# The gates of an mLSTM layer as float32 products in column quarters, moved from behind val(0) to behind the plain tiles

## The chip, the cores and the metric

The kernel runs on one NeuronCore of one Trainium2 chip. Its engines are TensorE (PE in the profile; PEld is its weight load), VectorE (DVE), ScalarE (ACT), GpSimd (POOL) and the queue engine SyncE (SP), which here issues nearly all transfers. The metric is the device time of one execution in microseconds. The kernel before has a median of 2676.51 us over three runs (2673.63 to 2676.99).

## The reference

One inference step of a decoder layer, for a prompt of 1024 rows and a group of 8 sample rows (1032 columns in the kernel, which keeps everything transposed), width 1024, all in float32:

```
x = LN1(ALPHA*x + 0.5*SwiGLU_1(x))
z = x @ w_in + b_in        # columns: q k v o-gate | i-gate(4) f-gate(4) | B C h | merge gates a, b
log_i = z[i-gate];  log_f = log_sigmoid(z[f-gate])
y_a = (HeadLN(mLSTM(q, k, v, log_i, log_f)) * sigmoid(o)) @ w_a
y_b = (B * conv3(C * h)) @ w_b
x = LN2(ALPHA*x + (sigmoid(g_a)*y_a + sigmoid(g_b)*y_b) @ w_mix)
x = LN3(ALPHA*x + 0.5*SwiGLU_2(x));  x = LN4(ALPHA*x + sigmoid(x @ w_pg) * (p @ w_pp))
```

The mLSTM is the chunked, stabilised form: cumulative sums of log_f, running maxima and exponentials of them weight the products of q, k and v. The part that this document is about is small: eight columns of z (four input gates, four forget gates), and the arithmetic that turns them into the decay factors of all chunks and heads.

## The kernel before, in words

Large products are done in the split form: each float32 operand is held as a high part in float32r and a low part, and a product is three float32r matmuls, high x high, high x low, low x high (L172 to L174 for plain tiles, L432 to L434 for the others). The 1032 columns are cut into four blocks (BLK4) of 256, 260, 256 and 260; most weights are taken in pairs of 128-column tiles, and such a pair is computed by a seven-product scheme (`pair`, L438) over two column halves: 14 steps of 12 matmuls each, with sums of x parts (`xsums`, L219) and of weight parts (`wcomb`, L249) prepared on DVE, ACT and POOL. After each step, `pair` takes one entry off the list `beside` (L436, L481) and issues what is in it: so small work of other kinds is threaded through the pairs.

All engines work in order. Which order that is, a planner of the framework decides when the kernel is built: it walks the program with a cost model and puts on each engine what is ready, by priority in program order. Tiles with one name share a fixed number of buffers: `mm` 4, `pn` 1 and `aux` 3 PSUM tiles, `raw` 3 and `tmp` 4 SBUF tiles. `unit_ps` (L103) takes every fifth tile from `pn`, the others from `mm`. `sg_pair` (L752) hands out two pairs of large tiles in turn, and `slot()` (L132) the ring of nine weight slots.

The stage concerned follows the first feed-forward part. Lines L958 to L971 compute LN1 for the four column blocks in the order 0, 2, 1, 3; its rows `rp` stay in SBUF in float32 and are split into high and low parts. L974 to L981 compute the first q and k tiles plainly (16 units of 24 matmuls). Then x is stored (L984), the weights of the first pair are loaded and combined, and the sums of x are formed: those of the first half before conv(0), those of the second half (`late_sums`, L229) as the first four entries of `beside`. conv(0) (L1227) is three pairs (C, h and B) with a short convolution (`conv_y`, L927) between the second and the third; val(0) (L1228) is one pair, whose result is transposed block by block (L1043) and stored; then come the gates (L1057 to L1088); then conv(1), q, k, val and so on for three more heads.

The gates before: the eight weight columns are split into high and low parts, laid side by side into a 128-column weight tile (i high at 0, f high at 32, i low at 64, f low at 96), and multiplied with the split parts of x, 16 or 24 matmuls for a column block, 80 in all (L1083 to L1085). The blocks of x are read from the parts of the seven-product scheme, some as sums of two parts, hence 24. The result `g0` (100 rows used) is transposed (L808, L815), and the rows that belong to high and low weights are added (`both`, L800). `gate_math` (L797) is a generator: each of its steps issues a few small instructions, and 22 entries of `beside` run it, so that it stands beside conv(1), which follows. Its results are needed by `decays` (L1090, from `gscr`) behind conv(1), and later by the chunks and the sample rows. Two of its inputs and outputs go through DRAM (L887 gscr, L914 state_m, L923 and L924 sscr and wkb).

Float32 matmuls that are not split are in the kernel too: the mean and variance of LN (L385, L407), the cumulative sums of the gates (L848, L850), and the products of the sample rows with their state (L1202), which put four 128x32 weight tiles into the four column quarters of TensorE and sum the four row groups of the result by a product with a selection matrix `sel` (L1210).

Of the kernel before, what the change touches and what calls it, by code (L numbers as in the profile page):

```python
# [8 lines left out]
F32 = mybir.dt.float32  # L9
R = mybir.dt.float32r  # L10
I32 = mybir.dt.int32
AF = mybir.ActivationFunctionType
OP = mybir.AluOpType
PSUM = bass.MemoryType.PSUM

D = 1024
# [7 lines left out]
Q0, K0, V0, O0, I0 = 0, 1024, 2048, 3072, 4096  # L24
# [6 lines left out]
BN = (256, 260)  # L31
BM = 260
BLK4 = [(i // 2 * HW + i % 2 * BN[0], BN[i % 2]) for i in range(4)]
# [3 lines left out]
def F_(ap):  # L37
    return ap.bitcast(F32)


def ccol(c):

    return c // 4 * HW + c % 4 * 128
# [6 lines left out]
def smp(t):  # L50

    return v2(t)[:, :, 512:516]
# [6 lines left out]
def p24(t):  # L59
    return t.rearrange("p (b r) -> p b r", r=4)  # L60
# [3 lines left out]
def layer_kernel(ctx: ExitStack, tc: tile.TileContext, I, O):  # L64
    nc = tc.nc
    V, S, G, T, DQ = nc.vector, nc.scalar, nc.gpsimd, nc.tensor, nc.sync

    sb = ctx.enter_context(tc.tile_pool(name="sb", bufs=1))
    rawp = ctx.enter_context(tc.tile_pool(name="raw", bufs=3))
# [17 lines left out]
    def sreg(dt=F32):  # L87

        t = sb.tile([128, 8 * BM], dt, name="sreg", tag="sreg")
        if dt == F32:  # L90
            SR[:] = [t]
            SN["v"] = [[t[:, i * HW + c:i * HW + c + n] for c, n in BLK4[:2]] for i in range(4)]
        return t

    def tmp(n=BM):
        return tmpp.tile([128, BM], F32, name="tmp", tag="tmp")[:, :n]
# [3 lines left out]
    def mm(n=512):  # L100
        return psp.tile([128, 512], F32, name="mm", tag="mm", bufs=NMM)[:, :n]

    def unit_ps(n=512):  # L103

        turn["n"] += 1
        return mm(n) if turn["n"] % 5 else psp.tile([128, 512], F32, name="pn", tag="pn", bufs=1)[:, :n]
# [3 lines left out]
    def aux(n=512):  # L110
        return psp.tile([128, 512], F32, name="aux", tag="aux", bufs=7 - NMM)[:, :n]


    ident = sb.tile([128, 128], F32, name="ident")
# [17 lines left out]
    def slot():  # L132
        s = ring["slots"][ring["i"] % len(ring["slots"])]
        ring["i"] += 1
        return gen(s, R)
# [47 lines left out]
    def bs(t, b, blk=BLK):  # L183
        c0, n = blk[b]
        return t[:, c0:c0 + n]
# [16 lines left out]

    def xparts(X7, j, kp):
        t = X7[j][kp // 2]
        return t[:, 2 * (kp % 2)], t[:, 2 * (kp % 2) + 1]
# [139 lines left out]
    def bcol(c0, m):  # L345
        return col(c0 // 128 + m) if c0 < 4096 else col(32 + (c0 - CB0) // 128 + m)
# [89 lines left out]
    beside = []  # L436
# [299 lines left out]
    w_in = I["w_in"][0]  # L736
    XP = x7()
# [14 lines left out]
    def sg_pair():  # L752
        if count["step"] == 0:
            return fixed
        i = 2 * (count["sg"] % 2)
        count["sg"] += 1
        return [gen(psgs[i + q]) for q in range(2)]
# [12 lines left out]
    ps = aux()  # L770
# [3 lines left out]
    ps = aux()  # L774
# [14 lines left out]
    def sg(shape, name):  # L789
        return sb.tile(shape, F32, name=name)  # L790
# [3 lines left out]
    wkb = sg([128, 8, 2, 4], "wkb")  # L794
    ems = sg([8, 4], "ems")

    def gate_math(gz, R_):  # L797
        gt = R_[0][:, :324].rearrange("p (c k) -> p c k", k=36)

        def both(dst, ps):  # L800

            V.tensor_copy(dst, ps[..., 0:36])
            V.tensor_tensor(dst, dst, ps[..., 64:100], op=OP.add)

        for q in range(2):
            ps = aux(400).rearrange("p (c k) -> p c k", k=100)
            for c in range(4):
                T.transpose(ps[:, c], gz[0:100, ccol(4 * q + c):ccol(4 * q + c) + 128], ident[:100, :100])  # L808
            yield
            both(gt[:, 4 * q:4 * q + 4, :], ps)  # L810
            yield
        gzs = R_[1][0:100, 0:8]
        V.tensor_copy(p24(gzs), smp(gz[0:100, :]))
        ps = aux(100)[0:8]
        T.transpose(ps, gzs, ident[:100, :100])  # L815
        yield
        V.memset(gt[:, 8, :], 0.0)
        both(gt[0:8, 8, :], ps)
        yield
        iv, fv = gt[:, :, 0:4], gt[:, :, 32:36]  # L820
        z = R_[1]

        def z9(i):
# [150 lines left out]
    for c in (0, 2, 1, 3):  # L974
        for k in range(2):
            for i in range(2):
                if len(wp) < 4:
                    wp.append(wcol(w_in, (Q0, K0)[k] + i * 128))
                ps = unit_ps(BLK4[c][1])
                unit(ps, wp[2 * k + i], [xplain(XP[c % 2], c, m) for m in range(8)])  # L980
                S.activation(bs(qk[k][i], c, BLK4), ps, AF.Identity, scale=(1.0, 1.0 / 16.0)[k], bias=bcol((Q0, K0)[k], i))  # L981
    sreg()
    for m in range(8):
        DQ.dma_start(x2scr[m], rp[m])  # L984
# [9 lines left out]
    def conv(jj, w=None):  # L994
        pre_ = sg_pair()

        def out_c(i, c, fn):
            fn(bs(pre_[i], c, BLK4))

        pair(w or in_pair(CC0 + jj * 256), XP, (0, 1), out_c, w is not None)  # L1000
        for i in range(2):
            S.activation(pre_[i], pre_[i], AF.Identity, bias=bcol(CC0, 2 * jj + i))

        def out_h(i, c, fn):
            d, t = bs(pre_[i], c, BLK4), tmp(BN[c % 2])
            fn(t)
            V.scalar_tensor_tensor(d, t, bcol(CH0, 2 * jj + i), d, op0=OP.add, op1=OP.mult)

        pair(in_pair(CH0 + jj * 256), XP, (0, 1), out_h)
        y = sg_pair()  # L1010
        for i in range(2):
            conv_y(2 * jj + i, pre_[i], y[i])

        def out_b(i, c, fn):
            d, t = bs(y[i], c, BLK4), tmp(BN[c % 2])
            fn(t)
            V.scalar_tensor_tensor(d, t, bcol(CB0, 2 * jj + i), d, op0=OP.add, op1=OP.mult)

        pair(in_pair(CB0 + jj * 256), XP, (0, 1), out_b)
        for i in range(2):  # L1020
            DQ.dma_start(yscr[2 * jj + i], y[i])
# [32 lines left out]
        V.tensor_copy(t, pt[0:8])  # L1054
        DQ.dma_start(vscr[h], t)

    def gates():  # L1057
        g0, g1 = sg_pair()

        graw = rawp.tile([128, 64], F32, name="raw", tag="raw").rearrange("p (k n) -> p k n", n=8)  # L1060
        DQ.dma_start(graw, w_in[:, I0:I0 + 8].rearrange("(k p) n -> p k n", p=128))
        s = slot()[:, :D]
        G.memset(F_(s), 0.0)

        gv = s.rearrange("p (k a b) -> p k a b", k=8, b=32)[:, :, :, 0:4]
        raw = graw.rearrange("p k (a b) -> p k a b", b=4)
        for k in range(8):
            S.copy(gv[:, k, 0:2], raw[:, k])
            V.tensor_tensor(gv[:, k, 2:4], raw[:, k], F_(gv[:, k, 0:2]), op=OP.subtract)
        gws = [s[:, k * 128:(k + 1) * 128] for k in range(8)]  # L1070
        gb = sb.tile([100, 1], F32, name="gb")
        V.memset(gb, 0.0)
        DQ.dma_start(gb[0:4, :], I["b_in"][0, I0:I0 + 4].rearrange("(p o) -> p o", o=1))
        DQ.dma_start(gb[32:36, :], I["b_in"][0, I0 + 4:I0 + 8].rearrange("(p o) -> p o", o=1))
        for c in range(4):
            X7 = XP[c % 2]
            ws, xs = [], []
            for k in range(8):
                for j in (((0,), (4, 0))[c // 2] if k < 4 else ((1,), (6,))[c // 2]):
                    ws.append(gws[k])  # L1080
                    xs.append(xparts(X7, j, k % 4))
            ps = mm(BN[c % 2])
            for i, (w, x) in enumerate(zip(ws, xs)):  # L1083
                for q in range(2):
                    T.matmul(ps, w, x[q], start=(i + q == 0), stop=(i == len(ws) - 1 and q == 1))  # L1085
            S.activation(bs(g0, c, BLK4)[0:100], ps[0:100], AF.Identity, bias=gb[:, :])
        steps = gate_math(g0, [g1[:, 0:324], g1[:, 324:584], g1[:, 584:968], g0[:, 0:257], g0[:, 260:516], g0[:, 520:648]])
        beside.extend([partial(next, steps, None)] for _ in range(22))  # L1088

    def decays(c0):  # L1090

        t = F_(slot())
# [35 lines left out]
    sgn = sg([8, 258], "sgn")  # L1128
    dn = sg([8, 4], "dn")
    dec = {}  # L1130
    sel = sg([128, 8], "sel")
    PS = sb.tile([128, 128], R, name="ps_")

    def smp_load(i, t):
# [23 lines left out]
    def dec_start():  # L1158
        c0, c1, c2 = gen(psgs[2]), gen(psgs[3]), gen(praws[0])
        dec["cd"] = [c[:, o:o + 512] for c in (c0, c1) for o in (0, 512)]  # L1160
        dec["vb"] = [c2[:, 0:256], c2[:, 256:512]]
        dec["qd"] = c2[:, 512:1024].rearrange("p (t a b) -> p t a b", t=2, b=32)
        G.memset(dec["qd"], 0.0)
        q8 = smp_load(0, F_(PS))
        V.tensor_tensor(sel, ident[:, 0:8], ident[:, 32:40], op=OP.add)
        for j in (64, 96):
            V.tensor_tensor(sel, sel, ident[:, j:j + 8], op=OP.add)
        dec["q"] = q8

    def dec_query(h):  # L1170
# [48 lines left out]
    def dec_end(h):  # L1219
# [3 lines left out]
        for dt in range(2):  # L1223
            y = ysm[:, 2 * h + dt]
            V.scalar_tensor_tensor(y, ph[:, dt * 8:dt * 8 + 8], gn(2 * h + dt), y, op0=OP.mult, op1=OP.mult)

    conv(0, w0)  # L1227
    val(0)  # L1228
    gates()
    for h in range(1, 4):  # L1230
        conv(h)
        if h < 3:
# [220 lines left out]
    ps = aux()  # L1453
# [377 lines left out]
```

## Time and profile before

| | |
|---|---|
| median of three runs | 2676.51 us |
| the profiled execution | 2676.36 us |
| its span, first to last instruction | 2674.6 us |
| granted TensorE clock, mean | 0.998 |
| PE busy | 2635.3 us, 21775 matmuls |
| DVE busy | 1840.7 us |
| ACT busy | 1272.1 us |
| POOL busy | 650.9 us |
| gate matmuls (L1085) | 80, from 829.4 to 840.3 us |

The profile is one execution. Records of matmuls overlap (a matmul of 256 columns is shown with 0.28 us, while the next one starts 0.12 us later), so the price of a matmul is read from the distance of starts in the timeline. A row of the timeline gives start, duration, engine, line, operation, the tile written and the tiles read, shape and, where rows are merged, their count; in brackets, idle time before it and what ended it. A row of the waits says who waited for whom, the time in all, how often, and the longest. Times in all views are microseconds from the start of the span.

### The profile page before, as it was taken

Reading aid. Unit: us, or ns where it says so; the run is one execution under the profiler, and the core shown is the slowest. Engines: PE = TensorE matmul, PEld = TensorE weight load, DVE = VectorE, ACT = ScalarE, POOL = GpSimd, SP = SyncE. Lnnn points to the kernel's source line nnn. Section 1 sums busy time; section 2 is a strip of 40 time slices with the busy share of each in tenths; the row PEclk is TensorE's granted clock in tenths of the full one; section 3 lists DMA queues with packets and bytes.
Section 4 is the critical chain, followed back from the end, with each engine's and each line's share of the span. In section 5 each row is a group of like instructions: output and inputs, shape, how many; then the busy total and the mean of one; then the engine's idle time right before and its main releaser. Section 6 shows DMA issues by size and latency. Waiting matters only on the chain.

```text
span 2674.6 us, 56234 instructions
## 1 busy us (share of the span) xinstructions
PE 2635.3 (99%) x21775; PEld 2597.2 (97%) x21775; DVE 1840.7 (69%) x4053; ACT 1272.1 (48%) x2774; POOL 650.9 (24%) x649
## 2 busy tenths in 40 slices
PE   9999999999999999999999999999999999999998
PEld 9999999999999999999999999999999999999888
DVE  6755556987885747555555678658855555888887
ACT  5544445433654444445566555426544444533351
POOL 2222221112431111111110335323322222111454
PEclk9999999999999999999999999999999999999999
DMA  6333235532233334336667676821423323643211
GB/s 208 104 108 102 89 108 185 180 121 68 88 116 96 116 100 125 90 90 191 197 193 240 220 245 210 258 80 51 155 88 108 107 87 107 219 148 117 86 51 58
DMA packets 311924, 355.15 MB, mean 133 GB/s; under 512 B 28536, under 2 KB 246344, under 8 KB 311656
## 3 DMA queue, kind: packets, MB, share of 16 engines
q1 hardware_dynamic: 289336, 330.30, 38.9%
q10 hardware_dynamic: 22320, 21.26, 2.7%
q8 instruction: 170, 2.79, 0.4%
q14 instruction: 98, 0.80, 0.1%
HBM read 246.09 MB, written 105.42 MB: 131 GB/s over the span
## 4 chain that ended last, share of the span: by engine, by line
PE 85%; DVE 7%; DMA 4%; issue 2%; ACT 2%; POOL 1%; SPq 0%; DVEq 0%; ACTq 0%; POOLq 0%
PE mm L432 15%; PE mm L433 14%; PE mm L434 14%; PE aux L432 6%; PE aux L434 6%; PE aux L433 6%; PE mm L172 5%; PE mm L174 5%; PE mm L173 5%; PE pn L172 1%; PE pn L174 1%; PE pn L173 1%; DVE a L212 1%; DVE a L589 1%; DVE a L612 1%
## 5 line engine op out<-in xcount | busy, mean ns | idle before, releaser
L432 PE MATMUL mm<-a,w 128*128 128x260 f32 (+1 forms) x2313 | 655.7, 284 | 3.0 <-DVE a L612 2.5
L433 PE MATMUL mm<-a,w 128*128 128x260 f32 (+1 forms) x2313 | 651.1, 282 | 0.9 <-DVE a L212 0.8
L434 PE MATMUL mm<-a,w 128*128 128x260 f32 (+1 forms) x2313 | 650.1, 281 | 0.0
L432 PEld LDWEIGHTS mm<-a,w 128*128 128x128 f32 x2313 | 435.3, 188 | 11.8 <-issue 8.7
L433 PEld LDWEIGHTS mm<-a,w 128*128 128x128 f32 x2313 | 435.7, 188 | 1.4 <-DVE a L212 1.3
L434 PEld LDWEIGHTS mm<-a,w 128*128 128x128 f32 x2313 | 435.3, 188 | 0.9 <-issue 0.8
L275 POOL TENSOR_TENSOR raw<-a,raw 128x512 f32<-128x512 f32 (+2 forms) x98 | 123.7, 1263 | 1137.4 <-issue 626.8
L259 DVE TENSOR_TENSOR w<-raw,w 128x512 fp32r<-128x512 f32 (+2 forms) x258 | 174.7, 679 | 198.2 <-ACT w L258 196.2
L432 PE MATMUL aux<-a,w 128*128 128x260 f32 (+1 forms) x1000 | 282.2, 282 | 0.2 <-DVE a L612 0.2
L434 PE MATMUL aux<-a,w 128*128 128x260 f32 (+1 forms) x1000 | 281.2, 281 | 0.0
L433 PE MATMUL aux<-a,w 128*128 128x260 f32 (+1 forms) x1000 | 281.1, 281 | 0.0
L432 PE MATMUL mm<-a,e 128*128 128x260 f32 (+1 forms) x785 | 222.4, 283 | 0.9 <-DVE a L612 0.9
L433 PE MATMUL mm<-a,e 128*128 128x260 f32 (+1 forms) x785 | 221.1, 282 | 1.1 <-DVE a L212 1.1
L434 PE MATMUL mm<-a,e 128*128 128x260 f32 (+1 forms) x785 | 220.9, 281 | 0.0
L174 PE MATMUL mm<-a,w 128*128 128x256 f32 (+3 forms) x739 | 208.1, 284 | 0.0
L172 PE MATMUL mm<-a,w 128*128 128x260 f32 (+4 forms) x695 | 198.5, 287 | 2.9 <-DVE a L647 1.7
L258 ACT CAST w<-a 128x512 fp32r<-128x512 f32 (+2 forms) x200 | 117.5, 588 | 171.4 <-PE mm L434 101.7
L173 PE MATMUL mm<-a,w 128*128 128x260 f32 (+4 forms) x695 | 197.4, 285 | 0.0
L432 PEld LDWEIGHTS aux<-a,w 128*128 128x128 f32 x1000 | 188.2, 188 | 2.6 <-issue 2.1
L433 PEld LDWEIGHTS aux<-a,w 128*128 128x128 f32 x1000 | 188.3, 188 | 0.0
L434 PEld LDWEIGHTS aux<-a,w 128*128 128x128 f32 x1000 | 188.2, 188 | 0.0
L258 ACT CAST w<-raw 128x512 fp32r<-128x512 f32 (+2 forms) x258 | 152.2, 591 | 67.2 <-PE aux L434 21.1
(543 smaller groups left out, 7645.9 us busy)
## 6 DMA issues: line engine op xcount, KB each, us to landing
a<-in_ffn_wi_dram SPq DMA_DIRECT2D x80, 512.0 KB
a<-in_w_in_dram SPq DMA_DIRECT2D x68, 512.0 KB
a<-hsum SPq DMA_DIRECT2D x119, 258.0 KB
hsum<-a SPq DMA_DIRECT2D x68, 258.0 KB
a<-in_ffn_wo_dram SPq DMA_DIRECT2D x40, 384.0 KB
a<-in_state_C_dram ACTq DMA_DIRECT2D x32, 256.0 KB
out_dram<-a ACTq DMA_DIRECT2D x32, 256.0 KB
raw<-in_w_b_dram SPq DMA_DIRECT2D x32, 256.0 KB
```

Of the source, the lines that this page charges most:

```text
L172: T.matmul(ps, wh, xh, start=(i == 0), stop=False)
L173: T.matmul(ps, wh, xl, start=False, stop=False)
L174: last = T.matmul(ps, wl, xh, start=False, stop=(i == n - 1))
L212: order_["lo"] = V.tensor_tensor(dst[1], src, F_(dst[0]), op=OP.subtract).ins
L258: S.copy(hi, src)
L259: V.tensor_tensor(lo, src, F_(hi), op=OP.subtract)
L275: G.tensor_tensor(s4, a12, s2, op=OP.subtract)
L432: T.matmul(ps, wh, xh, start=start and kp == 0, stop=False, skip_group_check=True)
L433: T.matmul(ps, wh, xl, start=False, stop=False, skip_group_check=True)
L434: T.matmul(ps, wl, xh, start=False, stop=stop and kp == len(xs) - 1, skip_group_check=True)
L589: V.tensor_tensor(lo, F_(lo), F_(hi), op=OP.subtract)
L612: V.tensor_tensor(r, r, ps, op=op)
```

## The change

The gates are computed straight behind the plain q and k tiles, before x is stored. For each column block, eight float32 matmuls take one 128-row tile of `rp` each; the weight tile is 128x32 (eight columns used, the rest zero), and the eight go to the four column quarters of TensorE in turn, two to a quarter, accumulating. So 32 float32 matmuls take the place of the 80 split ones. The result has 128 rows: four partial sums in four quarters, the bias added once. In `gate_math` the transpose becomes a product with `sel` (moved up), which turns the block and adds the four partial sums at once; the addition of high and low (`both`) goes, and the tile of gates shrinks from 36 to 8 columns a chunk. The 22 entries of `beside` are appended behind those of `late_sums`, so the arithmetic stands beside conv(0). `gates` no longer takes a ring slot and takes `sg_pair` one call earlier; each `gates` call takes a `unit_ps` tile in place of an `mm` tile.

```diff
+    sel = sg([128, 8], "sel")
+    V.tensor_tensor(sel, ident[:, 0:8], ident[:, 32:40], op=OP.add)
+    for j in (64, 96):
+        V.tensor_tensor(sel, sel, ident[:, j:j + 8], op=OP.add)
+    gb = sg([128, 1], "gb")
+    def gate_weights():
+        raw = rawp.tile([128, 64], F32, name="raw", tag="raw").rearrange("p (k n) -> p k n", n=8)
+        DQ.dma_start(raw, w_in[:, I0:I0 + 8].rearrange("(k p) n -> p k n", p=128))
+        gw = tmp(256).rearrange("p (k n) -> p k n", n=32)
+        G.memset(gw, 0.0)
+        S.copy(gw[:, :, 0:8], raw)
+        V.memset(gb, 0.0)
+        DQ.dma_start(gb[0:8, :], I["b_in"][0, I0:I0 + 8].rearrange("(p o) -> p o", o=1))
+        return gw
+    def gates(gw, g0, c):
+        ps = unit_ps(BLK4[c][1])
+        for m in range(8):
+            j = m % 4 * 32
+            T.matmul(ps[j:j + 32], gw[:, m], bs(rp[m], c, BLK4), start=(m < 4), stop=(m >= 4), tile_position=(0, j),
+                     skip_group_check=True)
+        S.activation(bs(g0, c, BLK4), ps, AF.Identity, bias=gb[:, :])
     def gate_math(gz, R_):
-        gt = R_[0][:, :324].rearrange("p (c k) -> p c k", k=36)
...
+        gt = R_[0][:, :72].rearrange("p (c k) -> p c k", k=8)
         for q in range(2):
-            ps = aux(400).rearrange("p (c k) -> p c k", k=100)
+            ps = aux(32).rearrange("p (c k) -> p c k", k=8)
             for c in range(4):
-                T.transpose(ps[:, c], gz[0:100, ccol(4 * q + c):ccol(4 * q + c) + 128], ident[:100, :100])
+                T.matmul(ps[:, c], gz[:, ccol(4 * q + c):ccol(4 * q + c) + 128], sel, start=True, stop=True)
             yield
-            both(gt[:, 4 * q:4 * q + 4, :], ps)
+            V.tensor_copy(gt[:, 4 * q:4 * q + 4, :], ps)
             yield
-        gzs = R_[1][0:100, 0:8]
-        V.tensor_copy(p24(gzs), smp(gz[0:100, :]))
-        ps = aux(100)[0:8]
-        T.transpose(ps, gzs, ident[:100, :100])
+        gzs = R_[1][:, 0:8]
+        V.tensor_copy(p24(gzs), smp(gz))
+        ps = aux(8)[0:8]
+        T.matmul(ps, gzs, sel, start=True, stop=True)
...
+    gw = gate_weights()
+    g0, g1 = sg_pair()
+    for c in (0, 2, 1, 3):
+        gates(gw, g0, c)
+    steps = gate_math(g0, [g1[:, 0:72], g1[:, 324:584], ...
     sreg()
     for m in range(8):
         DQ.dma_start(x2scr[m], rp[m])
...
-    def gates():
-        g0, g1 = sg_pair()
...
-        beside.extend([partial(next, steps, None)] for _ in range(22))
...
+    beside.extend([partial(next, steps, None)] for _ in range(22))
     conv(0, w0)
     val(0)
-    gates()
     for h in range(1, 4):
```

More of the change, by code (lines that the diff above doesn't have):

```diff
@@ L797, in gate_math @@
+    def gates(gw, g0, c):
[5 more added lines that the diff above has]
+        S.activation(bs(g0, c, BLK4), ps, AF.Identity, bias=gb[:, :])
     def gate_math(gz, R_):
-        gt = R_[0][:, :324].rearrange("p (c k) -> p c k", k=36)
-        def both(dst, ps):
-            V.tensor_copy(dst, ps[..., 0:36])
-            V.tensor_tensor(dst, dst, ps[..., 64:100], op=OP.add)
+        gt = R_[0][:, :72].rearrange("p (c k) -> p c k", k=8)
@@ L811, in gate_math @@
             yield
-        gzs = R_[1][0:100, 0:8]
-        V.tensor_copy(p24(gzs), smp(gz[0:100, :]))
-        ps = aux(100)[0:8]
-        T.transpose(ps, gzs, ident[:100, :100])
+        gzs = R_[1][:, 0:8]
+        V.tensor_copy(p24(gzs), smp(gz))
+        ps = aux(8)[0:8]
+        T.matmul(ps, gzs, sel, start=True, stop=True)
         yield
         V.memset(gt[:, 8, :], 0.0)
-        both(gt[0:8, 8, :], ps)
+        V.tensor_copy(gt[0:8, 8, :], ps)
         yield
-        iv, fv = gt[:, :, 0:4], gt[:, :, 32:36]
+        iv, fv = gt[:, :, 0:4], gt[:, :, 4:8]
@@ L981, in layer_kernel @@
                 S.activation(bs(qk[k][i], c, BLK4), ps, AF.Identity, scale=(1.0, 1.0 / 16.0)[k], bias=bcol((Q0, K0)[k], i))
+    gw = gate_weights()
+    g0, g1 = sg_pair()
+    for c in (0, 2, 1, 3):
+        gates(gw, g0, c)
+    steps = gate_math(g0, [g1[:, 0:72], g1[:, 324:584], g1[:, 584:968], g0[:, 0:257], g0[:, 260:516], g0[:, 520:648]])
     sreg()
@@ L1055, in val @@
         DQ.dma_start(vscr[h], t)
-    def gates():
-        g0, g1 = sg_pair()
[L1060 to L1087, printed above, removed]
-        beside.extend([partial(next, steps, None)] for _ in range(22))
     def decays(c0):
@@ L1130, in layer_kernel @@
     dec = {}
-    sel = sg([128, 8], "sel")
     PS = sb.tile([128, 128], R, name="ps_")
@@ L1164, in dec_start @@
         q8 = smp_load(0, F_(PS))
-        V.tensor_tensor(sel, ident[:, 0:8], ident[:, 32:40], op=OP.add)
-        for j in (64, 96):
-            V.tensor_tensor(sel, sel, ident[:, j:j + 8], op=OP.add)
         dec["q"] = q8
```

## Prediction

> **What bounds the kernel now.** I began with the head of the page and its busy times.
>
> ```profile
> span 2674.6 us, 56234 instructions
> PE 2635.3 (99%) x21775; PEld 2597.2 (97%) x21775; DVE 1840.7 (69%) x4053; ACT 1272.1 (48%) x2774; POOL 650.9 (24%) x649
> ```
>
> TensorE (PE) issues nearly without a break, so a matmul that disappears is worth what it kept PE from issuing, and a matmul that is added costs the same. The duration of a record is no price here, since records overlap; prices below are distances between starts. The timeline of PE at the place to which the gates move, then the busy times of the stages touched (start:end, length, then PE, PEld, DVE, ACT, POOL), then the waits of PE from 747 to 830 and from 829 to 900:
>
> ```profile
> 746.56 0.29 PE L174 MATMUL mm<-a,w 128*128 128x260 f32 x1
> 746.68 0.28 PE L432 MATMUL mm<-a,w 128*128 128x256 f32 x1
> ```
>
> ```profile
> 747.00:787.00 40.00, 38.84 (x321) 38.10 (x320) 32.34 (x61) 21.97 (x50) 12.34 (x11) 1.00 0.36 100
> 829.00:841.00 12.00, 12.00 (x104) 11.95 (x103) 4.05 (x11) 5.16 (x14) 0.00 (x0) 1.00 0.59 186
> 841.00:884.00 43.00, 42.71 (x355) 41.69 (x353) 27.35 (x89) 18.61 (x42) 5.15 (x4) 1.00 0.18 55
> 884.00:900.00 16.00, 15.32 (x127) 15.09 (x128) 15.67 (x35) 7.63 (x15) 1.28 (x1) 1.00 0.30 84
> ```
>
> ```profile
> PE mm L433 <- DVE a L212: 1.1, 2, 0.9
> ```
>
> ```profile
> PE mm L432 <- DVE tmp L470: 0.8, 1, 0.8
> ```
>
> The last plain tile (L174, 746.56) is followed 0.12 us later by the first product of conv(0) (L432): there is no hole for the gates to fill, and what they cost goes on PE's path. The second thing to see is VectorE (DVE): 32.34 of 40 us in conv(0)'s first two pairs, where PE waited 1.1 us for the late sums (L212), against 27.35 of 43 in conv(1), beside which the gate arithmetic stands now.
>
> **The change part by part.** *Removed: 80 gate matmuls* (16, 24, 16 and 24 by the loop at L1075 to L1085). The PE timeline has a long run of them:
>
> ```profile
> 829.87 3.45 PE L1085 MATMUL mm<-a,e 128*128 128x256 f32 x27
> 833.15 0.38 PE L1043 MATMUL aux<-ident,a 128*128 128x128 f32 x2
> ```
>
> 27 of them fill 833.15 - 829.87 = 3.28 us, 0.1215 each: 80 x 0.1215 = 9.7 us. The transposes of val(0) that are threaded between them stay; conv(1)'s first pair takes over as their company.
>
> *Removed: nine transposes of the gates (L808, L815).*
>
> ```profile
> 841.83 0.51 PE L808 MATMUL aux<-ident,a 100*128 100x100 f32 x4
> 842.12 0.37 PE L432 MATMUL mm<-a,e 128*128 128x260 f32 x1
> 842.32 0.28 PE L433 MATMUL mm<-a,e 128*128 128x260 f32 x1
> ```
>
> Four take 0.29 us and push the next ordinary step from 0.12 to 0.20: 0.37 a group. Two groups and a ninth transpose at a quarter of one: 0.83. Removed in all: 10.5 us.
>
> *Added: 32 float32 matmuls in column quarters.* The same form is in the trace, L1202 (128x32 weights, 256 columns, four quarters; one float32 matmul leaves two records). First a group of one matmul, then one of four, then a full-width float32 matmul (L385):
>
> ```profile
> 1234.26 0.28 PE L434 MATMUL mm<-a,w 128*128 128x256 f32 x1
> 1234.46 0.62 PE L1202 MATMUL pn<-a,a 128*32 128x256 f32 x2
> 1235.01 0.39 PE L432 MATMUL mm<-a,w 128*128 128x260 f32 x1
> 1235.24 0.28 PE L433 MATMUL mm<-a,w 128*128 128x260 f32 x1
> ```
>
> ```profile
> 1442.58 0.28 PE L434 MATMUL mm<-a,w 128*128 128x260 f32 x1
> 1442.79 0.64 PE L1202 MATMUL pn<-a,a 128*32 128x256 f32 x8
> 1443.36 0.39 PE L432 MATMUL mm<-a,w 128*128 128x256 f32 x1
> 1443.58 0.28 PE L433 MATMUL mm<-a,w 128*128 128x256 f32 x1
> ```
>
> ```profile
> 648.61 0.28 PE L173 MATMUL mm<-a,w 128*128 128x256 f32 x1
> 648.73 0.59 PE L385 MATMUL aux<-a,onesm 128*128 128x256 f32 x2
> 648.97 0.47 PE L174 MATMUL mm<-a,w 128*128 128x256 f32 x1
> 649.28 0.28 PE L172 MATMUL mm<-a,w 128*128 128x256 f32 x1
> ```
>
> One quarter alone: 1235.24 - 1234.26 = 0.98, less two ordinary steps of 0.12, is 0.74 us. Four quarters: 1.00 - 0.24 = 0.76. So four run in the time of one. At full width: 0.67 - 0.24 = 0.43. The 0.33 between is the price of going into the quarters and back. One `gates` call has two such rounds, four calls have eight. Low bound: one block, 8 x 0.43 + 0.33 = 3.8. Calls apart from each other: 4 x (2 x 0.43 + 0.33) = 4.8. Every round for itself: 8 x 0.76 = 6.1. All are ready together and stand in sequence, so they should stay together but for waits for a PSUM buffer; I take 4.3.
>
> The Trainium skill, "TensorE: Matmul & The Clock Gate", Measured speedup vs the span model, gives 2.38 times for three column tiles, not three times; at that efficiency the sum would be 32 x 0.43 / 3.2 = 4.3 us plus the switch, an estimate from that page; the trace shows better than that (0.76 against 0.74). "TensorEngine Tiling (Array Packing)", Key Properties, says that changing the mode drains TensorE; the 0.33 agrees, and by this rule a scattering of the 32 would be the danger.
>
> *Added: nine selection products* with gz as 128x128 float32 weights and eight moving columns. Nearest is L848 (128x128 float32 weights, 32 columns) with L850 behind it:
>
> ```profile
> 859.11 0.28 PE L432 MATMUL mm<-a,w 128*128 128x256 f32 x1
> 859.23 0.30 PE L848 MATMUL aux<-a,a 128*128 128x32 f32 x2
> 859.46 0.22 PE L850 MATMUL aux<-a,ones 128*1 128x32 f32 x2
> 859.61 0.38 PE L433 MATMUL mm<-a,w 128*128 128x256 f32 x1
> 859.84 0.28 PE L434 MATMUL mm<-a,w 128*128 128x256 f32 x1
> ```
>
> Four records in 0.73 - 0.24 = 0.49, 0.12 each; 18 records are 2.2 us (1.7 at the transposes' 0.09; 2.5 with a switch for the eight-column one). PE's own sum: -10.5 + 4.3 + 2.2 = **-4.0 us**, between -5.0 and -1.9.
>
> *Moved: the start of conv(0).* The chain of waits runs through this place so (the late sums follow):
>
> ```profile
> 746.88 0.49 ACT a L981
> 747.37 0.24 SPq L954
> 747.70 3.01 DMA kscr<-a
> ```
>
> The late sums wait for the store of k (it frees their tiles), not for PE. While PE does 4.3 us of gates this chain runs on, and the 1.1 us that PE waited for L212 is spent on gates instead: -1.1.
>
> *Moved: the gate arithmetic*, from beside conv(1) to beside conv(0), behind the four late sums in the same list. Waits of DVE from 841 to 900, and the first and last instruction of the arithmetic on DVE (some 50 of them, 12.4 us busy by the groups of these lines):
>
> ```profile
> DVE w L1098 <- DMA w<-gscr: 3.2, 1, 3.2
> DVE a L832 <- ACT a L831: 1.8, 1, 1.8
> ```
>
> ```profile
> 842.62 0.29 DVE L802 COPY a<-aux 128x144 f32<-128x144 f32 x1
> 876.80 0.18 DVE L910 TENSOR_SCALAR g<-g 128x32 f32<-128x32 f32 x1
> ```
>
> conv(1) gets these back: gscr is written a stage earlier, DVE no longer stands 3.2 us for it, and the 0.8 us that PE waited behind it (L470) should go: -0.8. conv(0) has to carry some 11.3 us (12.4 less the additions that fall away) where 40 - 32.34 = 7.7 us of DVE were idle; the gates' 4.3 us of PE add to that, so 12 us of room for 11.3, in part unusable, since DVE works in sequence and stands when one of these steps waits (1.8 us for the exponential, L831). Queued behind such a wait are the weight splits and PSUM evacuations that PE needs. Bounds: 0, and all 11.3. I take **2.0**, nearer to nothing, because PE has buffers ahead (five PSUM tiles) and pair steps of 1.4 us to absorb small delays.
>
> Smaller moves at nothing: the load of the gate weights and bias (two small transfers on SP's queue, ahead of x2scr's stores and conv(0)'s weight loads, which wait behind them if they are late), one of four `tmp` buffers held by gw until the gates are over, four activations (as before), eight weight splits less on ACT and DVE. Their cover is the q and k tiles, which PE works on up to 746.56; without it the last LN block or the loads would hold PE up, and I allow a pair step of 12 matmuls, 1.4 us. conv(0)'s first output goes to the tiles of rows 6 and 7 of x, so its evacuation waits for the third late sum; three aux buffers cover that, else it is a pair step again. Both are in the range.
>
> Sum: -4.0 - 1.1 - 0.8 + 2.0 = -3.9. From the profiled execution's 2676.36 us (0.15 below the median 2676.51): **2672.5 us**.
>
> **The rivals.** (a) DVE takes all arithmetic in idle time, the rounds form one block, the products cost 1.7: -10.5 + 3.8 + 1.7 - 1.9 = -6.9, **2669.5**. For it: conv(0) starts 4 us later while DVE runs on. Against: what DVE idles in that stage are mostly waits in a chain, which other work can fill only where it is ready.
>
> (b) Slower: conv(0) becomes DVE's. Most of the 11.3 us and the waits inside the arithmetic (1.8 on L831) come on PE as late weights and late evacuations, about 12 us: -5.9 + 12 = +6, **2682.5**. It decides once the crowding passes 5.9 us. For it: 32.34 of 40 us, and PE already waits there. Against: from 884 to 900 DVE is busy 15.67 of 16 us and PE still issues 15.32.
>
> (c) The change doesn't do what it says: the quarters do not run side by side, or the order scatters them, 32 x 0.43 + 0.33 = 14.1 us instead of 4.3: -3.9 + 9.8 = +5.9, **2682**. Against: 0.76 beside 0.74 above.
>
> (d) No change: val(0) loses the gates as its cover, and DVE's backlog eats the rest; PE's 4 us come back as waits at L1043 and in the first pairs of conv(1): **2676**. Against: DVE has only 4.05 us of work in the 12 of that stage.
>
> **How the numbers follow.** Forecast 0.47 (its own range 2670 to 2675.5), (a) 0.20, (b) 0.14, (c) 0.04, (d) 0.15. About 0.2% (5.3 us) can be told from no change. Faster by more: (a) and the lower end of the forecast, 0.32. Slower by more: most of (b) and (c), 0.14. Within: 0.54. The range 2666 to 2682 reaches to (b)'s threshold and below (a), since the planner orders everything behind this place anew.
>
> **What would show it.** Right: 64 records of the new gates in at most four groups with 3.8 to 4.8 us between the neighbours' starts; conv(0)'s first product near 751; no wait on L212; no wait on gscr. Wrong: groups of two records scattered; PE waits of over 6 us between 751 and 800 released by DVE; a new wait at val(0)'s transposes.

## The result, and the profile after

The changed kernel takes 2668.54 us (median of 13 runs, 2665.27 to 2675.12) against 2675.79 us for the kernel before on the same chip (13 runs, 2671.98 to 2678.89). The ratio is 0.9976, 95% interval 0.9969 to 0.9984: 7.3 us less by the medians, 6.4 us by the ratio. That is within the range on record (2666 to 2682), but below the forecast's own range (2670 to 2675.5), beside rival (a) with its 2669.5: by the ratio the gain is 1.6 times the 3.9 us that were forecast.

The head of the page after, with its span and the busy times; the span of before was 2674.6 us:

```profile
span 2666.8 us, 56196 instructions
PE 2629.8 (99%) x21768; PEld 2590.0 (97%) x21768; DVE 1832.3 (69%) x4042; ACT 1272.6 (48%) x2767; POOL 649.4 (24%) x649
```

PE's timeline after, at the place to which the gates were moved:

```profile
745.26 0.28 PE L174 MATMUL mm<-a,w 128*128 128x260 f32 x1
745.47 1.93 PE L819 MATMUL mm<-a,tmp 128*32 128x256 f32 x32
747.22 1.06 PE L819 MATMUL pn<-a,tmp 128*32 128x260 f32 x16
748.10 1.06 PE L819 MATMUL mm<-a,tmp 128*32 128x260 f32 x16
749.09 0.39 PE L432 MATMUL mm<-a,w 128*128 128x256 f32 x1
749.31 0.28 PE L433 MATMUL mm<-a,w 128*128 128x256 f32 x1
```

The 64 records stand in one block. From the last plain tile to the second product of conv(0) it is 4.05 us; less two ordinary steps of 0.12 us, the gates cost 3.81 us.

The windows after, with the columns of before's (start:end, length, PE, PEld, DVE, ACT, POOL), then the waits of PE from 747 to 830; from 829 to 900 that view lists none:

```profile
747.00:787.00 40.00, 38.38 (x339) 36.40 (x332) 31.23 (x80) 22.72 (x52) 11.51 (x11) 1.00 0.31 87
841.00:884.00 43.00, 42.99 (x363) 42.76 (x363) 25.59 (x57) 19.15 (x40) 5.17 (x4) 1.00 0.31 89
884.00:900.00 16.00, 16.00 (x137) 15.96 (x136) 15.83 (x38) 6.05 (x12) 4.16 (x2) 1.00 0.29 85
```

```profile
PE mm L432 <- ACT sreg L450: 0.9, 1, 0.9
PE aux L890 <- DVE a L887: 0.6, 1, 0.6
```

PE now issues through all of conv(1) (42.99 of 43 us and 16.00 of 16). In conv(0) the wait on L212 is gone and two others have come.

To compare kernels I use one stretch of PE's timeline: from the start of the last plain tile (L174) to the first transposes of val(1). Single executions reach its start up to 2.5 us apart for reasons that lie ahead of the change (747.39 and 744.87 us in two kernels below that are the same up to there), and a distance within one execution leaves these out. Its end in the kernel before, and in the one after:

```profile
965.18 0.71 PE L1043 MATMUL aux<-ident,a 128*128 128x128 f32 x5
```

```profile
958.06 0.71 PE L1068 MATMUL aux<-ident,a 128*128 128x128 f32 x5
```

Before: 965.18 - 746.56 = 218.6 us. After: 958.06 - 745.26 = 212.8 us, so 5.8 of the 7.8 us between the two spans lie here. The last plain tile itself comes 1.3 us earlier, and the other 0.7 us fall behind the stretch; both are of the size by which executions differ.

### The profile page after: what moved, and what is told of

The parts are those of the page before. It is cut to its first block, busy times and chain, and to the rows that moved or that the text cites. A ratio compares the mean times of both kernels' runs of the same rounds, so it can differ in the third digit from the quotient of the medians.

```text
span 2666.8 us, 56196 instructions
## 1 busy us (share of the span) xinstructions
PE 2629.8 (99%) x21768; PEld 2590.0 (97%) x21768; DVE 1832.3 (69%) x4042; ACT 1272.6 (48%) x2767; POOL 649.4 (24%) x649
## 4 chain that ended last, share of the span: by engine, by line
PE 87%; DVE 6%; DMA 3%; ACT 2%; issue 2%; POOL 1%; SPq 0%; DVEq 0%; ACTq 0%; POOLq 0%
PE mm L432 15%; PE mm L434 15%; PE mm L433 15%; PE aux L432 6%; PE aux L434 6%; PE aux L433 6%; PE mm L172 5%; PE mm L174 5%; PE mm L173 5%; PE pn L174 1%; PE pn L172 1%; PE pn L173 1%; DVE a L589 1%; DVE a L212 1%; DVE a L612 1%
## 5 line engine op out<-in xcount | busy, mean ns | idle before, releaser
L432 PE MATMUL mm<-a,e 128*128 128x260 f32 (+1 forms) x777 | 219.7, 283 | 0.4 <-DVE a L612 0.4
L433 PE MATMUL mm<-a,e 128*128 128x260 f32 (+1 forms) x777 | 218.7, 282 | 0.0
L434 PE MATMUL mm<-a,e 128*128 128x260 f32 (+1 forms) x777 | 218.5, 281 | 0.0
L172 PE MATMUL mm<-a,w 128*128 128x256 f32 (+4 forms) x743 | 212.6, 288 | 5.3 <-ACT w L1321 2.0
L173 PE MATMUL mm<-a,w 128*128 128x256 f32 (+4 forms) x743 | 210.1, 284 | 0.0
L174 PE MATMUL mm<-a,w 128*128 128x256 f32 (+4 forms) x697 | 196.7, 285 | 0.0
```

Source lines behind the costliest of these rows:

```text
L172: T.matmul(ps, wh, xh, start=(i == 0), stop=False)
L173: T.matmul(ps, wh, xl, start=False, stop=False)
L174: last = T.matmul(ps, wl, xh, start=False, stop=(i == n - 1))
L432: T.matmul(ps, wh, xh, start=start and kp == 0, stop=False, skip_group_check=True)
L433: T.matmul(ps, wh, xl, start=False, stop=False, skip_group_check=True)
L434: T.matmul(ps, wl, xh, start=False, stop=stop and kp == len(xs) - 1, skip_group_check=True)
```

## The experiments

All ratios are to the kernel before on the same chip, with 95% intervals; "stretch" is the distance just described.

**The changed kernel again.**

> The changed kernel once more, as the yardstick of this set on the same chip: 0.9976 of the kernel before, some 2669 us.

Measured: 2669.24 us, ratio 0.9979 (0.9970 to 0.9988), stretch 212.2 us. So one kernel's stretch repeats within 0.6 us.

**Form alone.** The new products at the old place, with their weights in a ring slot and their sums in `mm` tiles, as the kernel before has them:

```
     conv(0, w0)
     val(0)
+    gw = gate_weights()      # from behind the plain tiles
+    g0, g1 = sg_pair()
+    for c in range(4):
+        gates(gw, g0, c)     # F_(high half of split x) in place of rows
+    steps = gate_math(g0, [...])
+    beside.extend([partial(next, steps, None)] for _ in range(22))
```

> The new form (32 float32 quarter matmuls, nine selection products) at the old place, behind val(0), with the gate arithmetic beside conv(1) as before. It multiplies with the high halves of the split x of the first two blocks alone, since the float32 rows are gone there, so its gates are not the reference's; the number and the shape of its products are those of the change. Theory A (the gain is the sum of PE's shorter work, some 4.3 us by the distances in the two traces, and of stalls that go with the place, some 2 us, so each part shows by itself): -4.3 us, made up to 1.3 us smaller where val(0)'s transposes stand between the quarters (0.33 us for each switch): -3.0 to -4.3, ratio 0.9984 to 0.9989. Theory B (all of it comes from the place; the form is worth nothing): ratio 1.000. Theory C (all of it comes from the form): -6.4 us, ratio 0.9976.

Measured: 2677.32 us, ratio 1.0007 (0.9998 to 1.0016), stretch 218.9 us. PE's products did get shorter, but nothing is left of it at the end of conv(1). The waits of PE in this kernel, its timeline around the longest of them, and three windows (PE's granted clock is the number behind POOL):

```profile
PE mm L432 <- DVE tmp L470: 2.0, 1, 2.0
PE mm L433 <- DVE a L212: 0.9, 1, 0.9
PE aux L432 <- DVE g L925: 0.8, 1, 0.8
```

```profile
882.30 0.28 PE L434 MATMUL aux<-a,w 128*128 128x260 f32 x1
884.54 0.39 PE L432 MATMUL mm<-a,cd 128*128 128x256 f32 x1 [1.96 <-DVE tmp L470]
```

```profile
880.00:884.50 4.50, 1.80 (x13) 1.49 (x12) 4.50 (x16) 2.96 (x8) 0.00 (x0) 1.00 0.31 117
885.40:888.80 3.40, 3.40 (x18) 3.40 (x18) 3.40 (x9) 0.37 (x1) 0.00 (x0) 0.51 0.34 117
888.80:892.00 3.20, 3.20 (x29) 3.20 (x29) 2.60 (x5) 2.30 (x4) 0.00 (x0) 0.98 0.49 145
```

PE waits 0.8 and 2.0 us behind VectorE, and then takes 0.22 us a step and not 0.12 for 3.4 us, at a granted clock of 0.51: 18 instructions where 29 fit in the window behind. VectorE's side, from its timeline and its waits in the same kernel:

```profile
875.98 0.19 DVE L922 TENSOR_TENSOR g<-a 128x32 f32<-128x32 f32 x1
879.41 0.35 DVE L1085 SCALAR_TENSOR_TENSOR w<-w,ga,maskb 128x128 f32<-128x128 f32 x1 [3.23 <-DMA w<-gscr]
```

```profile
DVE w L1085 <- DMA w<-gscr: 3.2, 1, 3.2
```

VectorE works in sequence and stands until 879.41 for the decays' read of gscr, which the arithmetic has just written; in the kernel before it stood until 880.22 for the same (the row with 3.23 us on w<-gscr is its counterpart). Counted from the last plain tile (747.39 and 746.56), that end moved by only 1.6 us, from 133.7 to 132.0, while PE's own work had become some 4 us shorter. So theories A and C missed. The number of theory B, 1.000, came out, but the next kernel speaks against its reason: the place alone is worth nothing either.

**Placement alone.** The old form (split weights, transposes, two additions) behind the plain tiles:

```
-    val(0)
-    gates()
+    gws, gb = gate_weights()       # old weights, hi and lo in 100 columns
+    for c in (0, 2, 1, 3):
+        gates(gws, gb, g0, c)      # 16 products a block on the split x of the plain tiles
...
+    beside.extend([partial(next, steps, None)] for _ in range(22))
     conv(0, w0)
     val(0)
```

> The old form (split weights in 100 columns, transposes of the gates, two additions for each) right behind the plain tiles, arithmetic beside conv(0). It takes the parts of x that the plain tiles use, 64 matmuls in place of 80. Theory A: gates 64 x 0.1215 = 7.8 us and val(0)'s transposes without them 2.15 us, against 11.48 us for both together before, -1.5; stalls -2.0; sum -3.5 us, ratio 0.9987. Theory B (place alone): -6.4 us, ratio 0.9976. Theory C (form alone, and conv(0) pays the crowding of 2.0 us that the forecast had): -1.5 + 2.0 - 1.9 for the waits of L212 and L470 = -1.4 us, ratio 0.9995; the trace then shows PE waiting for DVE between 751 and 800 us.

Measured: 2675.95 us, ratio 1.0004 (0.9995 to 1.0013), stretch 219.8 us. Again nothing: 0.9987 (A) and 0.9976 (B) lie outside the interval, and 0.9995 (C) at its edge. PE's waits between 744 and 830 us come to 4.3 us in the view, 1.6 of them on the late sums (L212), where the changed kernel lists 1.5 in all. The parts are not additive: +0.2 and +1.2 us apart, -5.8 us together, by the stretches.

**No column quarters.**

```
-            j = m % 4 * 32
-            T.matmul(ps[j:j + 32], gw[:, m], ..., tile_position=(0, j), ...)
+            T.matmul(ps[0:32], gw[:, m], ..., start=(m == 0), stop=(m == 7))
```

> The changed kernel without column quarters: all eight float32 products of a block accumulate in the first 32 rows of PSUM, one behind the other, and the selection products take 32 rows in place of 128. Theory A (four quarters run in the time of one): 32 x 0.43 + 0.33 = 14.1 us in place of 3.8, +10.3 us beside the changed kernel, ratio 1.0015 to the kernel before. Rival (the 32 matmuls would be as cheap one behind the other, and the quarters add nothing): the same as the changed kernel, 0.9976.

Measured: 2679.98 us, ratio 1.0015 (1.0006 to 1.0024), stretch 223.1 us. PE's timeline in this kernel:

```profile
745.51 0.28 PE L174 MATMUL mm<-a,w 128*128 128x260 f32 x1
745.72 7.09 PE L818 MATMUL mm<-a,tmp 128*32 128x256 f32 x32
...
759.99 0.28 PE L433 MATMUL mm<-a,w 128*128 128x256 f32 x1
```

The gates take 759.99 - 745.51 - 0.24 = 14.2 us in place of 3.8. Theory A holds: the quarters run side by side.

**The decays half a stage later**, in the form-alone kernel and in the kernel before:

```
         conv(h)
-        if h < 3:
-            decays(4 * h - 4)
         lin(qscr, Q0, h, AF.Identity, sm=0)
         if h < 3:
-            decays(4 * h - 2)
+            decays(4 * h - 4)
         lin(kscr, K0, h, AF.Identity, 1.0 / 16.0, 1)
+        if h < 3:
+            decays(4 * h - 2)
```

> The new form at the old place again, with one thing moved: the decays, which read gscr back, are called half a stage later (behind the q and k tiles of each head, not ahead of them). Theory A2 (the shorter gates of the form-alone kernel were given back in conv(1), since the arithmetic's way through gscr has a length of its own and VectorE stands 3.2 us for it with evacuations queued behind): the waits of 0.93 and 2.12 us behind L925 and L470 go, and so does the low clock behind them (20 steps at +0.1 us, 2.0 us): -5.0 us beside the form alone, ratio to the kernel before 0.9987 to 0.9990. Theory D (conv(1) is VectorE's by its work, not by that wait): at most the decays' own 2.3 us of VectorE move, and PE goes on waiting: ratio 1.0000 to 1.0007.

> The kernel before with the decays called half a stage later and nothing else. Theory A2: only the waits of conv(1) go, 0.91 + 0.37 + 0.2 us = 1.5 us, ratio 0.9994. Rival (the late decays are worth as much here as with the short gates, so the gates' form has no part in it): -5 us, ratio 0.9981.

Measured: with the form 2672.55 us, ratio 0.9989 (0.9980 to 0.9997), stretch 214.3 us; without it 2673.42 us, ratio 0.9993 (0.9984 to 1.0002), stretch 216.7 us. From 841 to 925 us PE's waits list no entry in either kernel. The window of conv(1) in the one with the form:

```profile
841.00:884.00 43.00, 43.00 (x355) 42.00 (x355) 28.96 (x93) 18.62 (x40) 5.15 (x4) 1.00 0.13 39
```

One move that touches none of the gates brings 4.6 us back to the form-alone kernel (218.9 to 214.3) and 1.9 us to the kernel before (218.6 to 216.7). VectorE is busier in this window than in the form-alone kernel (28.96 us against 25.60) and yet PE waits for nothing, so theory D falls. One thing stays open: the move takes the decays' own 2.3 us of VectorE out of the place as well as the wait of 3.2 us, and their shares aren't told apart. With the read out of the way the form is worth 216.7 - 214.3 = 2.4 us of the stretch. The intervals of the two runs overlap, so the 2.4 us rest on the traces.

**Placement alone, with its weights in another tile.**

```
-        s = slot()[:, :D]                       # the ring of conv(0)'s weights
+    gws, gb = gate_weights(gen(psgs[1], R)[:, :D])
```

> The old form right behind the plain tiles, as in the placement-alone kernel, but its split weights in the tile that the arithmetic takes later, and not in a slot of the ring of conv(0)'s weights. Theory A2 (there VectorE stood 5.9 us for a weight tile, the late sums behind it began 5.7 us after conv(0) and not 2.4, and PE waited 2.4 us on L211, L212 and the evacuations behind them more than with the new form): the late sums begin within 3 us of conv(0)'s start, PE's stalls of 5.6 us fall to about 2.5, ratio 0.9991 to 0.9994. Rival (the old form itself crowds conv(0): its additions and transposes): as the placement alone, 1.0004.

Measured: 2678.09 us, ratio 1.0007 (0.9999 to 1.0016), stretch 220.8 us; VectorE stood as long for a weight tile as in the placement-alone kernel (5.94 us, 5.88 there). My reason was wrong: the ring's slot is not what holds conv(0). The issues of conv(0)'s weight loads (L245) on SP's queue show what does; first the changed kernel, then this one:

```profile
721.75 0.42 SPq L245 DMA_DIRECT2D a<-in_w_in_dram  x1
724.56 1.07 SPq L245 DMA_DIRECT2D a<-in_w_in_dram  x1
```

```profile
748.13 14.39 SPq L245 DMA_DIRECT2D a<-in_w_in_dram  x4
```

```profile
SPq L245 <- PE mm L819: 0.9, 1, 0.9
```

The loads that leave at 721.75 in the changed kernel leave at 748.13 here, and the queue's own waits name the gate products (L819 in this kernel). conv(0)'s first raw weights go to tiles 31 and 32 (`praws`), which hold the split x of block 2 (`parts`). The old products read the split x, the new ones the rows. VectorE then stood 5.94 us for a weight tile, with the late sums behind it:

```profile
752.39 1.46 DVE L259 TENSOR_TENSOR w<-a,w 128x512 fp32r<-128x512 f32 x1 [5.94 <-ACT w L258]
...
759.20 1.09 DVE L212 TENSOR_TENSOR a<-tmp,a 128x260 fp32r<-128x260 f32 x3
```

**The new products on the split x.** This tests that reading, with one operand exchanged:

```
-            T.matmul(ps[j:j + 32], gw[:, m], bs(rp[m], c, BLK4), ...)
+            T.matmul(ps[j:j + 32], gw[:, m], F_(xplain(XP[c % 2], c, m)[0]), ...)
```

> The changed kernel with one operand exchanged: the 32 quarter products read the high halves of the split x and not the rows (the low halves are left out, so the gates are not the reference's). Number, shape and place of the products stay. Theory A3 (conv(0)'s first weights go to tiles 31 and 32, which hold the split x of block 2; products that read them hold the weight loads back until the gates have run, and reading the rows sets these tiles free some 20 us earlier): the weight loads come behind the gates, past 746 us, VectorE stands for them, the late sums begin late, and PE's stalls in conv(0) rise by 2.5 to 4 us: ratio 0.9988 to 0.9993. Rival (the old form's own work, its splits, transposes and additions, made the stalls of the two placement kernels): nothing changes beside the changed kernel, 0.9976 to 0.9979.

Measured: 2674.36 us, ratio 0.9997 (0.9989 to 1.0006), stretch 217.1 us: 4.3 us over the changed kernel's, with the same products at the same place. In this kernel's SP queue the loads begin at 745.90, again behind the gate products (L819), and PE waits for them:

```profile
745.90 9.14 SPq L245 DMA_DIRECT2D a<-in_w_in_dram  x3
```

```profile
SPq L245 <- PE mm L819: 0.4, 1, 0.4
```

```profile
PE mm L432 <- ACT w L258: 2.9, 1, 2.9
PE mm L434 <- DVE w L259: 1.0, 1, 1.0
```

Theory A3 holds in kind, at slightly more than its 2.5 to 4 us, and this is shown, not only argued: which tile the products read decides most of the gain.

**More work on VectorE.**

```
+    def step_more():
+        next(steps, None)
+        for i in range(2):
+            V.tensor_copy(g1[:, ...126 columns], g1[:, ...])
-    beside.extend([partial(next, steps, None)] for _ in range(22))
+    beside.extend([step_more] for _ in range(22))
```

> The changed kernel with two copies of 128x126 more on VectorE in each of the 22 steps of the arithmetic (44 copies of some 0.25 us, about 11 us: the arithmetic once more). Theory A3 (VectorE has idle time left beside conv(0), 11.6 of 54.7 us from 745 to 800, and work in it is nearly free until that is used up): a loss of 1 to 4 us beside the changed kernel, ratio 0.998 to 0.999. Rival (the crowding was already at its limit, and each further us of VectorE is a us of PE): +8 to +11 us, ratio 1.0008 to 1.002.

Measured: 2670.82 us, ratio 0.9982 (0.9973 to 0.9991), stretch 213.7 us. It does not test what it was meant to: the planner put all 44 copies ahead of conv(0). The profile's row for their line:

```profile
L1219 DVE COPY a<-a x44: 210/221/787, 698.0 to 747.0; 128x126 f32<-128x126 f32 x44
```

How much more conv(0) could carry stays open.

**Scattered quarters**, two products at a time behind the plain tiles, into an `aux` tile:

```
                 S.activation(bs(qk[k][i], c, BLK4), ps, ...)     # a plain tile
+                gates(gw, g0, c, gp, 2 * k + i)                  # two of eight products
```

> The changed kernel with the quarter products given out behind the plain tiles, two at a time, and not in one block behind all of them; in its order 12 of them stand in one group and 20 in ten pairs. Theory A3 (a way into the quarters and back costs 0.33 us and a round of up to four 0.43): (3 x 0.43 + 0.33) + 10 x 0.76 = 9.2 us in place of 3.8, +5.4 us beside the changed kernel, ratio 0.9998. Rival (the 0.33 us is no price of the switch but of the float32 products' fill, hidden between plain tiles): at most the half-filled rounds show, +1 to +2 us, ratio 0.998 to 0.9985.

Measured: 2675.81 us, ratio 1.0007 (0.9998 to 1.0016). A pair in this kernel's timeline:

```profile
721.00 0.28 PE L174 MATMUL mm<-a,w 128*128 128x256 f32 x1
721.21 0.63 PE L818 MATMUL aux<-a,tmp 128*32 128x256 f32 x4
721.76 0.39 PE L172 MATMUL mm<-a,cd 128*128 128x256 f32 x1
721.99 0.28 PE L173 MATMUL mm<-a,cd 128*128 128x256 f32 x1
```

A pair costs 721.99 - 721.00 - 0.24 = 0.75 us, as a lone quarter or a whole round did before (0.74, 0.76); ten of them are 7.5 us. With the group of twelve, 1.7 us by the same count (1.6 expected), that is about 9.3 us where the block of 32 takes 3.8: +5.5, and theory A3 holds for the gates. The runs lost some 8. The rest is not settled; in the profiled execution a part of it is in a stage that the gates don't touch, the window of 1680 to 1720 us, where PE waited 3.0 us for one weight tile (0.7 in the changed kernel's window) and the mean clock fell to 0.91 (1.00 there):

```profile
1680.00:1720.00 40.00, 37.03 (x287) 36.55 (x286) 26.94 (x67) 16.79 (x32) 12.23 (x13) 0.91 0.88 274
```

```profile
PE mm L172 <- ACT w L148: 3.0, 1, 3.0
```

**Two tries at a better version.** In the first, the decode's products are held back in VectorE's order; the second adds two empty steps ahead of the arithmetic:

```
         if h == 3:
-            dec_pre()
+            with tc.issue_after(order_["lo"]):
+                dec_pre()
```

```
-    beside.extend([partial(next, steps, None)] for _ in range(22))
+    beside.extend([[] for _ in range(2)] + [[partial(next, steps, None)] for _ in range(22)])
```

> The changed kernel with the decode's first products (L1137) held behind VectorE's weight split of head 3, so that they are no longer hoisted into conv(0), where VectorE stood 3.2 us for wkb and PE 0.6 us for VectorE (L890). Theory A2: that wait goes, -0.7 us beside the changed kernel, ratio 0.9973 to 0.9976. Rival (VectorE's stand there costs nothing, since the chain of the arithmetic waits in any case): no change, 0.9976 to 0.9979.

> The changed kernel with the decode's first products held back to head 3 and the arithmetic begun two pair steps later, a try at a better version: of the stalls that are left in conv(0), 0.6 us on L887 go with the first edit, and the 0.92 us on L450, behind the exponential's table load and two activations, may go with the second. Theory A3: -1.0 to -1.5 us beside the changed kernel, ratio 0.9971 to 0.9974. Rival (the arithmetic only moves its stalls to other steps): 0.9976 to 0.9979.

Measured: 2669.24 us, ratio 0.9976 (0.9967 to 0.9985), stretch 211.9 us; and 2669.49 us, ratio 0.9981 (0.9972 to 0.9990), stretch 212.2 us. The wait on L887 is gone from the first, but 211.9 stands beside 212.2 to 212.8 for the changed kernel itself. The second only moved its stalls (0.7 us on L450, 0.3 on L457). Neither is better by anything that can be measured.

## Why the prediction was right, and where it was not

**What PE does: right.** -4.0 us was forecast. The gates and val(0)'s threaded transposes before run from a last ordinary step to the next:

```profile
828.81 0.28 PE L434 MATMUL mm<-a,w 128*128 128x260 f32 x1
828.94 0.71 PE L1043 MATMUL aux<-ident,a 128*128 128x128 f32 x5
...
840.41 0.28 PE L432 MATMUL mm<-a,e 128*128 128x256 f32 x1
```

That is 840.41 - 828.81 - 0.12 = 11.5 us. After, the same transposes alone cost 2.15 us (the sum over their groups from 835.67 to 845.64), so the 80 products were worth 9.3 us (9.7 forecast; by the loop the blocks take 16, 16, 24 and 24 of them, which leaves the sum as it was). The nine transposes of the gates made 0.8 to 0.9 (0.83 forecast). The quarters cost 3.81 (4.3, with 3.8 as the low bound: one block). The selection products:

```profile
756.20 0.28 PE L434 MATMUL mm<-a,w 128*128 128x256 f32 x1
756.31 0.95 PE L828 MATMUL aux<-sel,a 128*128 128x8 f32 x8
757.12 0.36 PE L432 MATMUL mm<-a,w 128*128 128x256 f32 x1
757.33 0.28 PE L433 MATMUL mm<-a,w 128*128 128x256 f32 x1
```

757.33 - 756.20 - 0.24 = 0.89 us a group, twice, and 0.3 for the ninth: 2.1 (2.2 forecast). Sum -4.3.

**conv(0): the crowding came as forecast, the relief was mis-sized.** +2.0 us was set against -1.1 for L212. By the distances between starts, PE's stalls in conv(0) were 2.1 us before, 1.8 of them on L212, and are 2.2 after, so the two terms together are +0.1 where +0.9 was forecast. The -1.1 came from the waits view, which leaves out the longer steps behind a wait. The wait on L212 went, as forecast: the store of k, for which the late sums wait, runs on while PE does the gates. ScalarE stood 1.8 us for it among them before (until 750.73, 4.1 us after conv(0)'s start), and 0.2 us after (until 751.65, 2.6 us after it). In its place the view has 0.9 us on L450 and 0.6 on L887. The second is released by VectorE, which itself stood 3.2 us for wkb there (a wait that the forecast didn't have). The first is released by ScalarE, but hangs on VectorE one step further back: ScalarE stood 2.4 us for VectorE's L470 and then had two activations of 1.2 us to do ahead of that copy. The arithmetic is about 11 us of VectorE here, from 749.7 to 799.0, and most of it went into idle time, if not all of it, as rival (a) said: from conv(0)'s start to the end of val(0) VectorE is busy 67.6 of 82.1 us, 63.7 in the kernel before, and 2.2 us of new stalls on PE are its price. (The windows from 747 to 787 don't show this, since 2 us of the one after still belong to the gates.)

**conv(1) and the rest.** -0.8 was forecast, again from the waits view and too small. The distances between starts give 1.5 us of stalls there before (a second wait, on L450, and the longer step behind each) and none after. The decays late in the kernel before show 1.9 us for the same place. What is left in VectorE's list from 841 to 900 is 0.7 us on the read of gscr, not 3.2. Two terms were missing: PE's other steps of the arithmetic cost 2.0 us beside conv(0) where they cost 2.4 beside conv(1), and a wait of 0.5 us on L407 ahead of the last plain tile is gone (what took it away isn't shown; it is back, with 0.8 us, in the kernel with more work on VectorE). Sum: -4.3 + 0.1 - 1.5 - 0.4 - 0.5 = -6.6. Without the last term, which lies ahead of the stretch, that is -6.1, beside 5.8 and 6.4 us less in the two executions of the changed kernel.

**The step that failed in kind.** The prediction added PE's shorter work and the stalls as independent terms, from the sentence that "a matmul that disappears is worth what it kept PE from issuing". The form-alone kernel shows that this does not hold by itself: some 4 us less work on PE came out as no less time (ratio 1.0007, 0.9998 to 1.0016; stretch 218.9 against 218.6), since the row with 3.2 us on gscr, priced at 0.8 us, grows into the bound when PE arrives earlier. It was right for the change as a whole because that also moves the arithmetic, so that the read lies a stage back. The second condition was not seen at all: the move is only free because the float32 products read the rows. "Smaller moves at nothing" looked at the buffers that the gates take, not at those that they keep others from; products on the split x cost 4.3 us of the stretch. That the sum came out in spite of this was luck: the edit happened to have what it needed.

**The rivals.** (a) came closest in the number and with its block of 3.8 us; its free arithmetic did not come true, and the larger relief in conv(0) and conv(1) made up for that. (b) falls: PE's new stalls in conv(0) are 2.2 us, not 12. (c) falls for the change, and its price was right (14.1 forecast, 14.2 in the kernel without quarters). (d) falls: val(0)'s transposes have no new wait, though without the gates between them the pairs stand alone at some 0.22 us each, inside the 2.15 above. Of the signs: one group, 3.81 us between the neighbours, no wait on L212. conv(0)'s first product came at 749.09 and not 751, as the whole program was 1.3 us early there and the gates 0.5 shorter.

## What to carry to other kernels

When a busy engine is made shorter, look for the chain beside it that does not get shorter (here a store and read-back through memory, on which an in-order engine stands), and ask what that wait becomes when the rest arrives earlier: its price today is only what shows today. When work is moved, list the tiles that it reads as well as those that it writes, and which transfers wait for them. Two edits that are each worth nothing can be worth something together, so undoing one at a time tells what they need from each other, not their shares.

## What the hardware showed beside this

**A stall of 2 to 3 us can cost twice.** In the form-alone kernel PE waited 0.8 and 2.0 us within 4.5 us and then ran 3.4 us at a granted clock of 0.51. In the kernel with products on the split x the same follows on waits of 2.9 and 1.0 us:

```profile
753.00:755.00 2.00, 2.00 (x10) 2.00 (x11) 2.00 (x4) 1.14 (x2) 0.00 (x0) 0.50 0.00 0
```

It doesn't take two waits. In the kernel before, in a later stage, one of 1.98 us was enough:

```profile
1699.85 0.39 PE L172 MATMUL mm<-a,e 128*128 128x256 f32 x1 [1.98 <-ACT e L148]
```

```profile
1701.80:1705.20 3.40, 3.40 (x18) 3.40 (x18) 2.02 (x6) 3.40 (x8) 0.73 (x1) 0.51 0.88 247
```

And it doesn't always follow: behind one of 3.10 us the changed kernel kept its full clock.

```profile
2550.47 0.70 PE L407 MATMUL aux<-sreg,onesm 128*128 128x256 f32 x2 [3.10 <-DVE sreg L404]
```

```profile
2550.40:2553.80 3.40, 3.33 (x24) 3.22 (x25) 2.43 (x8) 0.67 (x2) 0.00 (x0) 1.00 0.02 5
```

Waits of up to 1.4 us in conv(0) and conv(1) of these kernels had no such stretch behind them, even two of them within some 5 us (placement alone and its variant, 0.7 and 1.2 us). What decides between 2.0 and 3.1 us these traces don't show. The Trainium skill, "TensorE: Matmul & The Clock Gate", HAM oscillation, gives breaks of over some 3.4 us as the rule for the half clock; here shorter ones were enough, and the measurement decides.
